# A decoder trunk on one core: the first projection fed with the raw input, transposed in column halves, and the norm applied afterwards

## The chip, the core and the metric

The kernel runs on one core of a Trainium2 chip. A core has five engines that run their own instruction queues side by side: TensorE (PE) for matrix products and transposes, VectorE (DVE), ScalarE (ACT), GpSimd (POOL), and SyncE (SP), which here issues most of the DMA transfers. They wait for each other by semaphores. The metric is the device time of one execution in microseconds (us); less is better. The median of the runs is what is compared.

## The reference

Two layers work on a residual stream of 512 tokens by 1024 features in float32. The first is a sandwich-normed dilated attention (three groups of four heads), then a gated convolutional FFN; the second is a forgetting attention on keys and values made once, and another FFN. What matters here is the very first step:

```python
def rms_norm(x, g):
    x32 = x.astype(jnp.float32)
    y = x32 * lax.rsqrt(jnp.mean(x32 * x32, axis=-1, keepdims=True) + EPS)
    return (y * g.astype(jnp.float32)).astype(x.dtype)
...
    mix = dilated_mixer(rms_norm(h, g[0]), w_qkv_a[l], w_o_a[l], cos, sin)
...
def dilated_mixer(xn, w_qkv, w_o, cos, sin):
    B, T, _ = xn.shape
    qkv = xn @ w_qkv
    q, k, v = jnp.split(qkv, 3, axis=-1)
    q = apply_rope(q.reshape(B, T, A_HEADS, HEAD_DIM), cos, sin)
    k = apply_rope(k.reshape(B, T, A_HEADS, HEAD_DIM), cos, sin)
```

The norm divides each token (a row of x) by its root mean square and multiplies each feature (a column) by a gain. The product with `w_qkv` sums over features. So the gain has to be in before the product, while the division by the row's root mean square may be done before it or on the product's rows.

## The kernel before

Products in float32 precision are made of three matmuls in a rounded float32 format: each operand is split into a high part (a cast on ScalarE) and a low part (the value minus the high part, on VectorE), and high·high, high·low and low·high are summed in PSUM (`mm3`, lines 276 to 279). Weights come in pieces of 128 x 1024 numbers, 512 KB each; `Weights.load` issues the DMAs on SP, `high` and `low` make the parts (lines 57 and 65, tiles `wearly` or `wraw` to `w`), `split(n)` does so up to piece n, and `get` hands one out and splits some pieces ahead (`ahead`).

The order of all work is written out by hand: the program's lines are issued in the order of the text, and each engine takes its own instructions in that order. Tokens come in four blocks of 128. The first projection of group 0's queries and keys (`qk0`, 512 output columns, pieces 0 to 3 of two feature chunks each) goes as follows. For each block b, `load_x` brings 512 KB; `rstd_h` squares it on ScalarE (line 284), takes the root (286) and the reciprocal on VectorE (288); `normed` multiplies by this and by the gain (296); `transpose_in` makes eight transposes on TensorE (345) and splits the result into `xah` and `xal` (348, 349). The gain as a row is spread over all partitions by four matmuls with a row of ones (`gain0`, line 260). Nine matmuls on zeros (`warm_up`, line 238) stand ahead of the first real ones. `qk_post` copies a block's queries and keys out of PSUM (1087) and POOL turns them by the rotary table (1093 to 1096). `reorder` makes on POOL a second copy of the transposed input, `xph` and `xpl`, with tokens in strides of four, for groups 1 and 2 (1076).

Behind this come `v_proj0`, the values of group 0 (weight pieces 4 and 5, 256 columns, tile `v_ps`), between whose halves the queries and keys are transposed (`qk_transpose`, line 1102, tile `qkT_ps`) and scored, then the products of groups 1 and 2 (`wide_proj`) on the reordered copy with attention steps between, the output projection, and the FFNs and the second layer, which take most of the time. POOL works through rotations and reordering in the order of the text, so a rotation stands behind each reordering that is issued before it.

The order of the text for the first projection was: block 0's norm, piece 0 split, block 0's transposes, piece 1 split, then block by block with further norms, transposes and splits put between the products.

Of the kernel before, what the change touches and what calls it, by code (L numbers as in the profile page):

```python
# [28 lines left out]
ND = NF // 2  # L29
LAST = 3  # L30
# [3 lines left out]
class Weights:  # L34
# [18 lines left out]
    def high(self, minus=False):  # L53
        if self.n_split < len(self.pieces):
            self.load(self.n_split + 1 + self.ahead_dma)
            raw, pair = self.raw.pop(self.n_split), self.new_pair()
            self.nc.scalar.copy(pair[:, 0], raw)  # L57
            if minus:
                self.nc.scalar.activation(pair[:, 1], raw, AF.Copy, scale=-1.0)
            self.half_done.append((raw, pair))  # L60

    def low(self):
        if self.half_done:
            raw, pair = self.half_done.pop()
            self.nc.vector.tensor_tensor(pair[:, 1], raw, pair[:, 0].bitcast(F32), ALU.subtract)  # L65
# [36 lines left out]
def trunk_kernel(ctx, tc, x, norm_gains, w_qkv_a, w_o_a, w_q_b, w_o_b, kv_norm, w_kvf, b_f,  # L102
# [38 lines left out]
    for g in range(3):  # L141
        for s in range(4):
            def f(raw, g=g, s=s):
                v = raw.rearrange("p (k c) -> p k c", k=2)
                return [(v[:, :, 0:256], cols(wqkv, 2 * s, 2, g * 256, 256)),
                        (v[:, :, 256:512], cols(wqkv, 2 * s, 2, 768 + g * 256, 256))]
            add(f)
# [69 lines left out]
    def load_x(b):  # L217
        sp.dma_start(h[:, b, :], xv[b * 128:(b + 1) * 128, :])
# [8 lines left out]
    g_row = t4([1, D], name="g_row")  # L227
    sp.dma_start(g_row, norm_gains[0:1, 0, :])
    ones = sml.tile([1, 128], F32R, tag="ones", name="ones", bufs=1)
    dve.memset(ones.bitcast(F32), 1.0)  # L230
# [16 lines left out]
    load_x(3)  # L247
# [5 lines left out]
    gr = t4([1, D], F32R, name="gain_h"), t4([1, D], F32R, name="gain_l")  # L253
    dve.tensor_copy(gr[0], g_row)
    dve.tensor_tensor(gr[1], g_row, gr[0].bitcast(F32), ALU.subtract)
    gain0 = [bank([128, 512], name="gain00") for _ in range(2)]
    warm_up(4)
    for part in range(2):
        for i in range(2):
            pe.matmul(gain0[i], ones, gr[part][:, i * 512:(i + 1) * 512], start=part == 0, stop=part == 1)  # L260
    warm_up(5)
# [7 lines left out]
    same = cst.tile([128, 4], F32, name="same")  # L269
    dve.tensor_reduce(same, ident.rearrange("p (a c) -> p c a", c=4), axis=mybir.AxisListType.X, op=ALU.add)  # L270
    dve.tensor_scalar(same, same, -NEG, NEG, ALU.mult, ALU.add)
    dve.tensor_tensor(mask2.rearrange("p (a c) -> p a c", c=4),
                      mask0[:, 128:256].rearrange("p (a c) -> p a c", c=4),
                      same[:, None, :].to_broadcast([128, 32, 4]), ALU.add)

# [5 lines left out]
    def rstd_h(b):  # L281
# [5 lines left out]
        r = small(1, "rs")  # L287
        dve.reciprocal(r, sd)
        return r

    H2 = (slice(0, 512), slice(512, 1024))
# [777 lines left out]
    def reorder(*blocks):  # L1069

        for i in range(2):
            for b in blocks:
                for part in range(2):
                    src = by_fourth(xT[part][i][:, :, b * 128:b * 128 + 128])
                    dst = xP[part][i].rearrange("p k (r l) -> p k r l", r=4)[:, :, :, b * 32:b * 32 + 32]
                    pool.tensor_copy(dst, src.bitcast(F32))
# [6 lines left out]
    def qk_post(g, b, o):  # L1083
# [3 lines left out]
        act.copy(qk.rearrange("p a d -> p (a d)"), o)  # L1087
# [162 lines left out]
    def norm0(b):  # L1250
        xn[b] = normed(b, rstd_h(b), gain0)

    def transpose0(b):
        transpose_in(b, xn.pop(b), xT)

    def qk0(b, *pieces):
        if b not in qk_banks:
            qk_banks[b] = bank([128, T], name="qk_ps")
        for s in pieces:
# [3 lines left out]
            for k in range(2):  # L1263
                kc = 2 * s + k
                ah, al = ax(0, b, kc)
                mm3(qk_banks[b], ah, al, wh[:, k, :], wl[:, k, :], kc == 0, kc == KD - 1)
# [24 lines left out]
    qk0(2, 2, 3)  # L1291
    W.split(5)
    qk_post(0, 2, qk_banks[2])
    qk0(3, 0, 1, 2, 3)
    W.ahead = 4
    W.split(6)
# [3 lines left out]
    reorder(2, 3)  # L1300
# [20 lines left out]
    def v_post(g, b, o):  # L1321
# [3 lines left out]
        act.copy(V[1][:, b, :], o[:, 0:256])  # L1325
        dve.tensor_copy(V[2][:, b, :], o[:, 256:512])
# [582 lines left out]
```

## Time and profile before

| | |
|---|---|
| median of 3 runs | 1109.95 us (1109.84 to 1110.57) |
| the profiled execution | 1110.27 us |
| its span, first to last instruction | 1108.5 us |
| TensorE busy | 1098.4 us, 99% of the span |
| VectorE, ScalarE, POOL busy | 81%, 60%, 20% |
| mean granted TensorE clock | 0.998 |

In the profile's rows a time is the start in us from the span's start, followed by how long it took; `L277` is line 277 of the kernel; `out<-in` names the tiles; `xN` counts instructions; a bracket at the end names the idle time before and what ended it. In rows of groups the numbers behind the bar are the busy time, the mean of one in ns, and the idle time before. In rows of stretches (`A:B`) the first number is the length, then the busy time and the count for TensorE, TensorE's weight loads, VectorE, ScalarE and POOL, then the granted clock, the DMA share and GB/s. Busy time of TensorE counts its work on zeros too, and its matmuls overlap in these rows: one is shown with 0.39 us where the next starts 0.23 us later.

### The profile page before, as it was taken

What the parts mean: (1) busy time and instruction counts of PE and PEld (TensorE: products, weight loads), DVE (VectorE), ACT (ScalarE), POOL (GpSimd) and SP (SyncE); (2) the same over time, 40 slices, a digit from 0 to 9 for tenths busy, and PEclk for the clock granted to TensorE, in tenths of its full rate; (3) what the DMA queues carried; (4) which work ended last, traced back from release to release, by engine and by line L of the source; (5) the groups of instructions that cost most, each with busy time, mean ns of one, the idle gap of its engine ahead of it and who ended that gap; (6) DMA issues with size and microseconds to landing.
All of it is one profiled execution on the core that took longest, in us unless ns stands there. A gap on an engine that the chain in (4) does not pass through costs nothing.

```text
span 1108.5 us, 18139 instructions
## 1 busy us (share of the span) xinstructions
PE 1098.4 (99%) x6611; PEld 948.4 (86%) x6611; DVE 896.6 (81%) x1494; ACT 660.2 (60%) x1092; POOL 222.2 (20%) x329
## 2 busy tenths in 40 slices
PE   9999999999999999999999999999999999999997
PEld 6988889889999988888888787789989999988886
DVE  6577878978887799997877777858978887799995
ACT  5444566566565547476555677756565565547473
POOL 1832100211111111000010766600211111111000
PEclk9999999999999999999999999999999999999999
DMA  9469864467789989885872677584467779999872
GB/s 325 149 207 408 346 171 132 108 134 196 176 201 216 256 318 341 295 310 108 210 153 76 193 222 211 161 246 124 114 133 191 181 200 219 249 315 340 306 247 77
DMA packets 184563, 237.32 MB, mean 214 GB/s; under 512 B 11737, under 2 KB 131529, under 8 KB 183962
## 3 DMA queue, kind: packets, MB, share of 16 engines
q1 hardware_dynamic: 166970, 176.61, 49.0%
q0 software_dynamic: 17504, 59.55, 23.3%
q8 instruction: 52, 0.85, 0.3%
q14 instruction: 37, 0.30, 0.1%
HBM read 170.28 MB, written 39.63 MB: 189 GB/s over the span
## 4 chain that ended last, share of the span: by engine, by line
PE 89%; DVE 3%; issue 3%; ACT 2%; DMA 2%; POOL 1%; DVEq 0%; POOLq 0%; ACTq 0%
PE up L278 13%; PE up L277 13%; PE up L279 13%; PE acc L278 8%; PE acc L277 8%; PE acc L279 8%; PE qk_ps L278 2%; PE qk_ps L277 2%; PE qk_ps L279 2%; PE first L279 1%; PE first L277 1%; PE first L278 1%; PE o_ps L1762 1%; PE pT_ps L1747 1%; PE v_ps L278 1%
## 5 line engine op out<-in xcount | busy, mean ns | idle before, releaser
L277 PE MATMUL acc<-w 128*128 128x512 f32 (+1 forms) x311 | 120.5, 388 | 0.0
L279 PE MATMUL acc<-w 128*128 128x512 f32 (+1 forms) x311 | 120.4, 387 | 0.0
L57 ACT CAST w<-wraw 128x1024 fp32r<-128x1024 f32 x96 | 99.0, 1048 | 9.5 <-issue 3.9
L278 PE MATMUL acc<-w 128*128 128x512 f32 (+1 forms) x267 | 103.2, 387 | 0.0
L65 DVE TENSOR_TENSOR w<-wraw,w 128x1024 fp32r<-128x1024 f32 x66 | 88.1, 1356 | 15.1 <-ACT w L57 14.7
L641 ACT ACTIVATE bb<-up,conv 128x512 f32<-128x512 f32 x80 | 60.0, 776 | 67.3 <-DVE up L1022 42.8
L278 PE MATMUL up<-xbl,w 128*128 128x512 f32 (+1 forms) x280 | 96.3, 344 | 0.0
L278 PE MATMUL up<-xcl,w 128*128 128x512 f32 (+1 forms) x280 | 96.3, 344 | 0.0
L277 PE MATMUL up<-xch,w 128*128 128x512 f32 (+1 forms) x280 | 96.3, 344 | 0.0
L277 PE MATMUL up<-xbh,w 128*128 128x512 f32 (+1 forms) x280 | 96.3, 344 | 0.0
L279 PE MATMUL up<-xbh,w 128*128 128x512 f32 (+1 forms) x280 | 96.2, 344 | 0.0
L279 PE MATMUL up<-xch,w 128*128 128x512 f32 (+1 forms) x280 | 96.2, 344 | 0.0
L277 PE MATMUL up<-xsh,w 128*128 128x256 f32 x320 | 90.6, 283 | 0.0
L278 PE MATMUL up<-xsl,w 128*128 128x256 f32 x320 | 90.6, 283 | 0.0
L279 PE MATMUL up<-xsh,w 128*128 128x256 f32 x320 | 90.6, 283 | 0.0
L277 PEld LDWEIGHTS acc<-w 128*128 128x128 f32 x311 | 58.4, 188 | 12.0
L279 PEld LDWEIGHTS acc<-w 128*128 128x128 f32 x311 | 58.4, 188 | 11.8
L644 DVE SCALAR_TENSOR_TENSOR bb<-up,conv,bb 128x510 f32<-128x510 f32 x80 | 59.9, 749 | 2.8
L642 DVE SCALAR_TENSOR_TENSOR bb<-up,conv,bb 128x511 f32<-128x511 f32 x80 | 59.4, 742 | 2.6 <-ACT bb L641 2.6
L277 PEld LDWEIGHTS up<-xsh,w 128*128 128x128 f32 x320 | 61.4, 192 | 0.0
L278 PEld LDWEIGHTS up<-xsl,w 128*128 128x128 f32 x320 | 61.4, 192 | 0.0
L279 PEld LDWEIGHTS up<-xsh,w 128*128 128x128 f32 x320 | 61.4, 192 | 0.0
(337 smaller groups left out, 3161.2 us busy)
## 6 DMA issues: line engine op xcount, KB each, us to landing
wraw<-in_w_up_dram SPq DMA_DIRECT2D x88, 512.0 KB, 5.0
w<-wraw POOLq DMA_DIRECT2D x50, 512.0 KB, 6.1
dT<-dsums SPq DMA_DIRECT2D x24, 512.0 KB, 6.0
hD<-hc POOLq DMA_DIRECT2D x44, 256.0 KB, 7.6
dact<-hD SPq DMA_DIRECT2D x44, 256.0 KB, 5.2
wraw<-dT SPq DMA_DIRECT2D x22, 512.0 KB, 6.6
wraw<-in_w_down_dram SPq DMA_DIRECT2D x22, 512.0 KB
dsums<-in_w_down_dram SPq DMA_DIRECT2D x18, 512.0 KB, 5.6
```

Of the source, the lines that this page charges most:

```text
L57: self.nc.scalar.copy(pair[:, 0], raw)
L65: self.nc.vector.tensor_tensor(pair[:, 1], raw, pair[:, 0].bitcast(F32), ALU.subtract)
L277: pe.matmul(o, ah, bh, start=first, stop=False, skip_group_check=shared)
L278: pe.matmul(o, ah, bl, start=False, stop=False, skip_group_check=shared)
L279: pe.matmul(o, al, bh, start=False, stop=last, skip_group_check=shared)
L641: act.activation(bb[:, s, :], ps, AF.Identity, bias=cp[:, 3, ch:ch + 1], scale=cp[:, 2, ch:ch + 1])
L642: dve.scalar_tensor_tensor(bb[:, s, 1:], ps[:, :T - 1], cp[:, 1, ch:ch + 1], bb[:, s, 1:], ALU.mult, ALU.add)
L644: dve.scalar_tensor_tensor(bb[:, s, 2:], ps[:, :T - 2], cp[:, 0, ch:ch + 1], bb[:, s, 2:], ALU.mult, ALU.add)
L1747: pe.transpose(o[:, k0 + k, :], p[:, hh, k * 128:(k + 1) * 128], ident)
L1762: pe.matmul(o[64 * hh:64 * hh + 64, i * 128:(i + 1) * 128], Vt[hd // 8][:, k, (hd % 8) * 64:(hd % 8) * 64 + 64], pT[j, i, hh][:, k, :], st ...
```

## The change

The first projection now takes the raw input. x is loaded and transposed in column halves (`load_x(b, i)`, `transpose0(b, i)`: four transposes of `h` itself). The gain comes in as eight rows of 128 and is turned by one transpose into a column per feature chunk (`gain0`, 128 x 8). When a half-block leaves PSUM, the gain is applied as a scale per partition, one instruction of 128 x 128 for each of the four chunks on ScalarE (the high part) and on VectorE (the low part): `split0`. Each row's reciprocal root mean square goes into a column of `r0` (`rstd0`) and is applied where the products leave PSUM: in `qk_post`, in `v_proj0` and in `v_post`. Groups 1 and 2 need these scales in the strided token order, `r1`: POOL's queue writes `r0` to DRAM and reads it back.

The order is new as well. The first halves of all blocks and pieces 0 and 1 go first: the products of pieces 0 and 1 on blocks 0 to 3, then those of pieces 2 and 3. Within a piece the three products are ordered by operand and no longer by chunk. Pieces 0 and 1 are loaded and split in two halves by chunk. `reorder` is called by column half, the first half of all blocks ahead of all rotations, the second behind them. The four gain matmuls are gone, and the five later warm-up matmuls stand behind the first four transposes.

```diff
@@ class Weights
-            self.nc.scalar.copy(pair[:, 0], raw)
+            for s in HALVES[self.n_split < 2]:
+                self.nc.scalar.copy(pair[:, 0, s], raw[:, s])
...
-            self.nc.vector.tensor_tensor(pair[:, 1], raw, pair[:, 0].bitcast(F32), ALU.subtract)
+            for s in HALVES[self.n_split < 2]:
+                self.nc.vector.tensor_tensor(pair[:, 1, s], raw[:, s], pair[:, 0, s].bitcast(F32), ALU.subtract)
@@ loads
-    load_x(0)
+    load_x(0, 0)
+    sp.dma_start(g_rows, norm_gains[0, 0].rearrange("(k p) -> k p", p=128))
     W.load(2)
-    load_x(1)
+    load_x(1, 0)
+    load_x(2, 0)
+    load_x(3, 0)
     W.load(3)
-    load_x(2)
+    load_x(0, 1)
     W.load(4)
+    for b in range(1, 4):
+        load_x(b, 1)
@@ gain
-    gr = t4([1, D], F32R, name="gain_h"), t4([1, D], F32R, name="gain_l")
-    dve.tensor_copy(gr[0], g_row)
-    dve.tensor_tensor(gr[1], g_row, gr[0].bitcast(F32), ALU.subtract)
-    gain0 = [bank([128, 512], name="gain00") for _ in range(2)]
-    warm_up(4)
-    for part in range(2):
-        for i in range(2):
-            pe.matmul(gain0[i], ones, gr[part][:, i * 512:(i + 1) * 512], start=part == 0, stop=part == 1)
-    warm_up(5)
+    gain0 = sml.tile([128, 8], F32, tag="gain0", name="gain0", bufs=1)
+    warm_up(WARM[0])
+    g0_ps = bank([128, 8], name="g0_ps")
+    pe.transpose(g0_ps, g_rows, ident[:8, :8])
+    dve.tensor_copy(gain0, g0_ps)
@@ evictions
-        act.copy(qk.rearrange("p a d -> p (a d)"), o)
+        act.activation(qk.rearrange("p a d -> p (a d)"), o, AF.Copy, scale=scale_of(g, b))
...
-                act.copy(V[0][:, b - 1:b + 1, :], banks[b // 2])
+                for i in range(2):
+                    act.activation(V[0][:, b - 1 + i, :], banks[b // 2][:, i], AF.Copy, scale=scale_of(0, b - 1 + i))
@@ the first projection
+    def transpose0(b, i):
+        n = 2 if (b, i) == (0, 0) else 4
+        for k0 in range(0, 4, n):
+            pt = bank([128, n, 128], name="xt_ps")
+            for k in range(n):
+                c = (4 * i + k0 + k) * 128
+                pe.transpose(pt[:, k, :], h[:, b, c:c + 128], ident)
+                x_ps[b, 4 * i + k0 + k] = pt[:, k, :]
+
+    def split0(b, i, ks=range(4)):
+        s = slice(b * 128, b * 128 + 128)
+        parts = [(xT[0][i][:, k, s], xT[1][i][:, k, s], x_ps.pop((b, 4 * i + k)),
+                  gain0[:, 4 * i + k:4 * i + k + 1]) for k in ks]
+        for hi, lo, o, g in parts:
+            act.activation(hi, o, AF.Copy, scale=g)
+        for hi, lo, o, g in parts:
+            dve.scalar_tensor_tensor(lo, o, g, hi.bitcast(F32), ALU.mult, ALU.subtract)
...
+            for x, w in ((0, wh), (1, wh), (0, wl)):
+                for k in range(2):
+                    kc = 2 * s + k
+                    pe.matmul(o, ax(0, b, kc)[x], w[:, k, :], start=kc == 0 and x == 0 and w is wh,
+                              stop=kc == KD - 1 and w is wl)
...
-    norm0(0)
+    transpose0(0, 0)
+    warm_up(WARM[1])
+    split0(0, 0, (0, 1))
     W.split(1)
-    transpose0(0)
+    split0(0, 0, (2, 3))
     W.split(2)
     qk0(0, 0)
-    norm0(1)
+    x0(1, 0)
     qk0(0, 1)
+    x0(2, 0)
+    qk0(1, 0)
     W.split(3)
-    transpose0(1)
-    qk0(0, 2)
-    norm0(2)
-    qk0(1, 0)
+    qk0(1, 1)
+    x0(3, 0)
+    qk0(2, 0, 1)
     W.split(4)
-    qk0(1, 1, 2)
-    transpose0(2)
-    qk0(0, 3)
-    norm0(3)
-    qk0(1, 3)
+    x0(0, 1)
...
+    qk0(3, 0, 1)
+    x0(1, 1)
+    rstd0(0)
+    reorder(0, 3, 0, 1, 2)
+    qk0(0, 2, 3)
+    x0(2, 1)
     qk_post(0, 0, qk_banks[0])
+    qk0(1, 2, 3)
+    rstd0(1)
+    x0(3, 1)
+    W.split(5)
     qk_post(0, 1, qk_banks[1])
-    reorder(0, 1)
-    qk0(2, 0, 1)
-    transpose0(3)
+    rstd0(2)
     qk0(2, 2, 3)
-    W.split(5)
+    W.split(6)
+    rstd0(3)
     qk_post(0, 2, qk_banks[2])
-    qk0(3, 0, 1, 2, 3)
+    qk0(3, 2, 3)
     W.ahead = 4
-    W.split(6)
     qk_post(0, 3, qk_banks[3])
     sums = down_sums([(1, 6), (1, 7)], in_two, sp, 1, 3)
     next(sums)
-    reorder(2, 3)
+    pool.dma_start(rd.rearrange("(b p) o -> p (b o)", p=128), r0)
+    reorder(1, 0, 1, 2, 3)
+    pool.dma_start(r1, rd.rearrange("(l r) o -> l (r o)", r=4))
```

`x0(b, i)` is `transpose0(b, i)` followed by `split0(b, i)`; `WARM` is (4, 5); `HALVES` gives two halves of 512 columns for pieces 0 and 1 and the whole for the others. Rows without times in the prediction show the instructions as each engine's queue holds them, with the semaphores that they wait for.

More of the change, by code (lines that the diff above doesn't have):

```diff
@@ L226, in trunk_kernel @@
     dve.memset(eps_t, EPS)
[L227 to L230, printed above, removed]
+    g_rows = t2([8, 128], name="g0_rows")
     zero = t2([128, 512], BF16, name="zero")
@@ L286, in rstd_h @@
         act.activation(sd, ss, AF.Sqrt, bias=eps_t)
[L287 removed]
+        r = small(1, "rs") if r is None else r
         dve.reciprocal(r, sd)
         return r
[L291 removed]
     def normed(b, r, gain):
@@ L1067, in by_fourth, with scale_of, reorder @@
         return a.rearrange(spec, r=4)
[L1069 to L1076, printed above, removed]
+    r0 = sml.tile([128, 4], F32, tag="r0", name="r0", bufs=1)
+    r1 = sml.tile([128, 4], F32, tag="r1", name="r1", bufs=1)
+    rd = tc.dram_tile([T, 1], F32, name="rd")
+    def scale_of(g, b):
+        return (r1 if g else r0)[:, b:b + 1]
+    def reorder(i, *blocks):
+        for b in blocks:
+            for part in range(2):
+                src = by_fourth(xT[part][i][:, :, b * 128:b * 128 + 128])
+                dst = xP[part][i].rearrange("p k (r l) -> p k r l", r=4)[:, :, :, b * 32:b * 32 + 32]
+                pool.tensor_copy(dst, src.bitcast(F32))
     def ax(g, b, kc):
```

45 lines of the change are left out of this document (25 added, 20 removed).

## The prediction

> **What bounds the kernel now.** The page first: one engine carries the span.
>
> ```profile
> span 1108.5 us, 18139 instructions
> PE 1098.4 (99%) x6611; PEld 948.4 (86%) x6611; DVE 896.6 (81%) x1494; ACT 660.2 (60%) x1092; POOL 222.2 (20%) x329
> ```
>
> TensorE is busy for all but 10 us. So time can go only where it does no useful work, and the busy row hides such work at the start, where it runs on zeros. Then the chain of waits for the first 16 us, and the timeline around the hand-over from this projection to the value projection.
>
> ```profile
> 1.36 1.89 PE warm L238 x4
> 3.24 2.24 PE gain L260 x4
> 5.48 2.25 PE warm L238 x5
> 7.73 1.65 PE xt_ps L345 x8
> ...
> 9.42 0.46 issue
> 9.88 1.05 ACT w L57
> 10.94 1.05 ACT junk L284 x2
> ...
> 12.01 0.30 ACT sd L286
> ...
> 13.21 0.74 DVE xn L296
> 13.95 1.15 DVE w L65
> ...
> 15.14 0.50 PE qk_ps L278
> ```
> ```profile
> 9.28 0.50 PE L277 MATMUL qk_ps<-w,xah 128*128 128x512 f32 x1
> ...
> 20.53 1.03 PE L345 MATMUL xt_ps<-ident,xn 128*128 128x128 f32 x8
> ...
> 35.47 0.39 PE L278 MATMUL qk_ps<-w,xah 128*128 128x512 f32 x1
> 35.70 0.39 PE L279 MATMUL qk_ps<-w,xal 128*128 128x512 f32 x1
> 35.92 0.28 PE L277 MATMUL v_ps<-w,xah 128*128 128x256 f32 x1
> 36.04 0.28 PE L278 MATMUL v_ps<-w,xah 128*128 128x256 f32 x1
> ...
> 41.68 1.03 PE L1102 MATMUL qkT_ps<-ident,qk 128*128 128x128 f32 x8
> ```
> ```profile
> 15.20:36.10 20.90, 20.90 (x101) 17.45 (x102) 11.22 (x15) 9.40 (x17) 11.78 (x15) 1.00 0.73 241
> ```
>
> The reader is to see three things. Until 9.28 no matmul of the projection runs; until 15.14 the end is set by ScalarE and VectorE, which take turns at squares, norms and splits. From 15.2 to 36.1 (the row by itself: stretch, TensorE busy) TensorE is full. And the projection ends at 35.92, where the value projection starts; 5.76 us later, at 41.68, come the first transposes of queries and keys. From there on nothing stops TensorE until the tail, so what the first 36 us save is carried to the end, unless a new wait eats it.
>
> **The change part by part.** The work of the projection on TensorE stays: 96 matmuls of 512 columns, 0.2275 us apart (35.47 to 35.70, rounded), 21.84 us, and 32 transposes at about 0.11 us ((1.03 − 0.27) / 7). Reordering the three products inside a piece costs nothing by that rate. So the question is when the stream starts and what interrupts it.
>
> *Arrival of x.*
>
> ```profile
> 0.74 0.35 SPq L228 DMA_DIRECT2D g_row<-in_norm_gains_dram  x1
> 1.15 0.35 SPq L218 DMA_DIRECT2D h<-in_x_dram  x1
> 4.85 1.06 ACT L284 ACTIVATE junk<-h 128x1024 bf16<-128x1024 f32 x1 [2.61 <-DMA h<-in_x_dram]
> ```
> ```profile
> 2.50:5.00 2.50, 2.50 (x6) 0.99 (x4) 2.32 (x5) 0.15 (x1) 0.00 (x0) 1.00 0.85 308
> 10.00:16.00 6.00, 4.99 (x24) 3.52 (x24) 5.54 (x8) 5.06 (x8) 0.00 (x0) 1.00 1.06 378
> ```
>
> The first block, 512 KB, was issued at 1.15 and waited for until 4.85. Now half of it is asked for, 0.41 us earlier (in g_row's place, 0.74), and 256 KB less at 308 GB/s (last column) is 0.85 us: it is there at 3.6. The gain rows, 4 KB behind it, I put at 3.75. Behind them one transfer of 256 KB lands each 0.85 us at first, 0.7 later: the halves of piece 0 at 4.5 and 5.3, of piece 1 at 6.1 and 6.9, x of blocks 1 to 3 by 9. All 4.1 MB are in by about 15, as before; SP's three added issues of 0.35 us are faster than what they wait behind.
>
> *Start of TensorE.* These are the rows of order ahead of the first matmuls, before and now:
>
> ```order
> L260 MATMUL gain_116<-gain_h,ones 128x512 [waits DVE_49]
> L260 MATMUL gain_117<-gain_h,ones 128x512
> L260 MATMUL gain_116<-gain_l,ones 128x512 [waits DVE_49]
> L260 MATMUL gain_117<-gain_l,ones 128x512
> L238 LDWEIGHTS zero
> L238 MATMUL warm<-zero 128x512
> ...
> L345 MATMUL xt_ps<-ident,xn 128x128 [waits DVE_49,Pool_49]
> L345 MATMUL xt_ps<-ident,xn 128x128 x3
> ...
> L277 MATMUL qk_ps<-w,xah_146 128x512 [waits Activation_49]
> ```
> ```order
> L267 MATMUL g_ps<-ident,g_rows 128x8 [waits DMAHW1_49,Pool_49]
> L1263 MATMUL xt_ps<-ident,h 128x128 [waits DMAHW0_49]
> L1263 MATMUL xt_ps<-ident,h 128x128 x3
> L245 LDWEIGHTS zero
> L245 MATMUL warm<-zero 128x512
> ...
> L1290 MATMUL qk_ps<-w,xah_133 128x512 [waits Activation_49] x2
> L1290 MATMUL qk_ps<-w,xal_135 128x512 [waits DVE_49] x2
> L1290 MATMUL qk_ps<-w,xah_133 128x512 [waits DVE_49] x2
> L1263 MATMUL xt_ps<-ident,h 128x128 [waits DMAHW6_49]
> ```
>
> The gain broadcast (four matmuls, 2.24 us of the chain) and the wait for a normalized block leave; the raw transposes wait for a DMA alone and stand ahead of the five warm-ups. Early on TensorE runs at half its later rate:
>
> ```profile
> 5.42 2.31 PE L238 MATMUL warm<-zero 128*128 128x512 bf16 x5
> 7.53 1.84 PE L345 MATMUL xt_ps<-ident,xn 128*128 128x128 f32 x8
> ```
>
> Eight transposes span 1.84 us here and 1.03 at 20.53; warm-ups stand 0.43 apart, though the granted clock reads 1.00 throughout. By 9.28 the rate is full. So: gain transpose at 3.75, four transposes to 4.8, five warm-ups of 0.43 to 7.0. I take 7.05 for the first projection matmul. Before, full rate came some 3.8 us after the five warm-ups began (5.42); here that would be 8.6; I take 9.15, the place it had.
>
> Are its operands there? Prices:
>
> ```profile
> L1154 ACT COPY PT<-pT_ps x4: 266/278/299, 56.9 to 57.4; 128x128 f32<-128x128 f32 x4
> ```
> ```profile
> L821 ACT CAST w<-dt 128x512 fp32r<-128x512 f32 x22 | 13.6, 618 | 1.8 <-DMA dt<-dT 1.6
> ...
> L1113 ACT ACTIVATE p<-p,st 128x128 f32<-128x128 f32 x36 | 14.0, 394 | 9.0 <-DVE st L1112 8.9
> ...
> L534 ACT ACTIVATE xqh<-nT,gcol 128x512 fp32r<-128x512 f32 x8 | 5.1, 716 | 0.0
> ...
> L348 ACT CAST xah<-xt_ps 128x512 fp32r<-128x512 f32 x8 | 4.4, 589 | 7.9 <-PE xt_ps L345 7.9
> ```
> ```profile
> L535 DVE SCALAR_TENSOR_TENSOR xql<-nT,gcol,xqh 128x512 fp32r<-128x512 f32 x8 | 5.5, 747 | 0.0
> ...
> L1112 DVE CUSTOM_DVE_ANT_0 p<-s_ps,mask 128x128 f32<-128x128 f32 x36 | 8.0, 286 | 1.9 <-PE s_ps L1129 1.9
> ```
>
> No row is a 128x128 copy out of PSUM with a scale per partition. Below: a plain one stands about 0.17 us from the next (four start between 56.9 and 57.4). Above: 0.39 (L1113). The scale adds 0.10 (716 against 618), so I take 0.27, nearer to L1154, which is the same copy but for the scale; a half-block on ScalarE then costs 1.08 us where one cast cost 0.59. On VectorE one of the four takes between 0.2 (L1112, less its overlap) and 0.33; I take 0.26, 512-column L535 less 384 columns. A half piece is 0.52 there and 0.62 on VectorE, half of the chain's 1.05 and of the 1.22 below. With ScalarE free at 4.9, two splits, piece 0 and two more end at 7.2, piece 1 at 8.2; VectorE has the low part of piece 0 at 7.5 and of piece 1 at 9.3. TensorE wants them at 7.05, 8.8 and 10.7: all in time.
>
> *The stream.* From 7.05: 21.84 us of matmuls and 28 transposes, 3.05. Half rate until 9.15, as before: 2.1 us do 4.9 matmuls instead of 9.2, a loss of 1.0. One stall I find by going through the queues: block 1's transposes end at 9.8, ScalarE's four at 11.1, VectorE's four at 12.3, TensorE asks at 12.0: 0.3. Later half-blocks are ready 0.3 to 2 us ahead. Sum: 7.05 + 21.84 + 3.05 + 1.0 + 0.3 = 33.25, against 35.92: **2.65 us earlier**.
>
> *What moved behind it.* The squares and roots (10.94 to 12.31 in the chain, 1.35 us a block on ScalarE) now stand among late splits, ahead of the casts of pieces 4 and 5:
>
> ```order
> L1271 ACTIVATE xah_134<-xt_ps,gain_114 128x128 [waits PE_49]
> L1271 ACTIVATE xah_134<-xt_ps,gain_114 128x128 x3
> L60 CAST w<-wearly 128x1024 [waits DMAHW2_49]
> L1091 ACTIVATE qk_343<-qk_ps,r_141 128x512 [waits DVE_49]
> L284 ACTIVATE junk,s_393<-h 128x1024 [waits DMAHW7_49]
> L286 ACTIVATE sd<-s_393,eps_t 128x1 [waits Activation_49]
> L60 CAST w<-wearly 128x1024 [waits DMAHW3_49]
> ```
>
> This is ScalarE's queue now, near 29 us; before, both casts stood there without squares between. Piece 5 is cast by 33.0, its low part by 34.3; the value projection wants it after 12 matmuls of 0.12 us (35.92 to 36.04), at 34.8: covered by 0.5. On POOL the first halves' reordering (8 casts) goes ahead of all rotations, the second halves' behind them, with two small DMAs for the scales in the strided order, which the first grouped projection needs only after its last product, some 20 us later. The scaled evictions add about 0.1 us each on ScalarE, off the path. The masks' three small instructions fall into VectorE's idle time near 21.
>
> The sum is against the profiled execution, 1110.27; the median of the runs lies 0.32 lower, 1109.95. 1109.95 − 2.65 = **1107.3 us**.
>
> **A rule weighed.** The Trainium skill, "TensorE: Matmul & The Clock Gate", Part 1, says that the array starts at half rate and goes to full after a busy window of about 3.4 us whose phase is free. The rows above do not show it counted from 1.36, since 9.03 was still slow; counted from the warm-ups at 5.42 it fits. By that rule the full rate comes between 8.2 and 11.6 here (4.8 + 3.4, plus up to one window), and my sum would read 3.1 down to 1.8 us instead of 2.65.
>
> **The rivals.** *A, full rate comes before the first real matmul.* For it: nothing breaks the stream from 4.0 on. Against: before, TensorE was at work from 1.36 and still slow at 8.8. It gives back the 1.0: 1106.3.
>
> *B, half rate lasts until about 12.5.* Counted from 7.05, when the warm-ups end, 3.8 us lead to 10.9; counted from behind the transposes that break the stream (10.5 at half rate), to 14.3; I take the middle. Each us costs 0.47 (1 − 0.2275/0.43): 1.6 more, less the stall it hides: gain 1.4, 1108.6. For it: the gap from 3.25 to 3.75 and the short instructions; against: the warm-ups stand together as before. (The same page says, in Part 4, that transposes do not count as work for the clock; that would favour B.)
>
> *C, ScalarE becomes the bound.* At 0.39 a split the late half-blocks miss TensorE by 0.2 to 0.5, and if the low part of piece 5 takes 1.97 instead of 1.22, as one did beside POOL (below), the value projection waits 0.9: gain 1.0, 1108.95. Against: the PSUM copy row.
>
> *D, slower: the rotations come too late.* In place of rotations first, POOL's queue now starts with the reordering, ahead of the first block's rotation (tu):
>
> ```order
> L1080 CAST xph_137<-xah_133 128x16x32 [waits Activation_49]
> L1080 CAST xpl_139<-xal_135 128x16x32 [waits DVE_49]
> L1080 CAST xph_137<-xah_133 128x16x32
> L1080 CAST xpl_139<-xal_135 128x16x32
> ...
> L1097 TENSOR_TENSOR tu<-qk_343,rope 128x128 [waits DMAHW1_49,Activation_49]
> ```
> ```order
> L1096 TENSOR_TENSOR qk_302<-tu 128x8x16 [waits Pool_49]
> L1076 CAST xph_150<-xah_146 128x16x32
> L1076 CAST xpl_152<-xal_148 128x16x32 [waits DVE_49]
> L1076 CAST xph_150<-xah_146 128x16x32
> L1076 CAST xpl_152<-xal_148 128x16x32 [waits DVE_49]
> ```
> ```profile
> 13.86 1.22 DVE L65 TENSOR_TENSOR w<-wearly,w 128x1024 fp32r<-128x1024 f32 x1
> ...
> 29.55 1.97 DVE L65 TENSOR_TENSOR w<-wearly,w 128x1024 fp32r<-128x1024 f32 x1
> ```
> ```profile
> 28.27 1.13 POOL L1076 CAST xpl<-xal 128x512 fp32r<-128x512 f32 x1
> ...
> 30.37 2.12 POOL L1076 CAST xpl<-xal 128x512 fp32r<-128x512 f32 x1
> ...
> 38.05 1.30 POOL L1094 TENSOR_TENSOR tu<-qk,rope 128x64 f32<-128x64 f32 x1
> ```
>
> The first order fence is now: eight casts, then the rotations. The second is before: the rotations of blocks 0 and 1, then casts. A cast takes 1.1 us, and 2.1 while VectorE runs L65; rotation steps then take 1.3. If all paid the high price from 17.6 on: 8 × 2.1 + 8 × 1.3 = 27.2, the second block is turned at 44.8, while TensorE asks at 39.5: it stands 5.3 us, 1112.6. It decides from 42.2 on. Against: only weight splits showed that price, and few fall into this stretch; at the low price the second block is done by 33.
>
> **How the numbers follow.** The forecast's own case (gain 1.9 to 3.2) gets 0.50, A 0.18, B 0.13, C 0.08, D 0.05; 0.06 is for what I do not see, half of it slower. The range goes from A with data a little earlier still (gain 4.1, 1105.8) to B and C together (gain 0.4, 1109.6). A measurement of this kernel tells about 0.2%, 2.2 us, from no change; 1107.73 is that bound, and 0.35 of the forecast's 0.50 lies beyond it. Faster: 0.35 + 0.18 + 0.03 = 0.56; same: 0.15 + 0.13 + 0.08 = 0.36; slower: 0.05 + 0.03 = 0.08.
>
> **What would show it.** First projection matmul near 7.05, value projection at 33.3, first transposes of queries and keys at 39.05. Right for the clock: matmuls 0.43 apart until about 9.15. C would show as waits of value matmuls for VectorE's split, D as transposes waiting for POOL. Wrong altogether if the raw x lands no earlier than 4.8, or if a later stage opens waits that were not there.

## The result, and the profile after

The changed kernel takes 1106.95 us in the median (7 runs, 1106.44 to 1107.10), beside 1110.21 for the kernel before: a ratio of 0.997, 95% interval 0.996 to 0.9981. Measured again later, beside other runs of the kernel before, it took 1106.85 (0.9969, 0.9957 to 0.9981). The prediction was 1107.3. The gain is 3.3 us where 2.65 was forecast.

The head of the page of the changed kernel:

```profile
span 1105.0 us, 18176 instructions
PE 1096.0 (99%) x6608; PEld 948.5 (86%) x6608; DVE 894.8 (81%) x1510; ACT 667.4 (60%) x1120; POOL 222.7 (20%) x331
```

TensorE is still busy for all but 9 us, but with 2.4 us less of it. What has gone is the gain broadcast, four matmuls of 2.24 us, for which one short transpose of 0.24 came in (6608 matmuls instead of 6611). The nine matmuls on zeros are all still there, and so is the work of the projection. The chain of waits at the start (start, duration, what):

```profile
0.74 0.39 SPq L228
1.19 2.32 DMA g_rows<-in_norm_gains_dram
...
3.65 0.24 PE g_ps L267
3.89 1.05 PE xt_ps L1263 x4
4.94 2.13 PE warm L245 x5
7.07 2.56 PE qk_ps L1290 x6
9.63 0.52 PE xt_ps L1263 x4
10.15 1.38 PE qk_ps L1290 x6
...
11.97 2.76 PE qk_ps L1290 x12
```

Before, ScalarE and VectorE stood in this chain until 15.14. Now nothing but TensorE stands in it after the gain rows have landed. Six matmuls take 2.56 us at first and 1.38 from 10.15 on: that is the change from half to full rate. The trace's record of the granted clock puts it at 9.67; the record begins there, so that stretches before it are shown with 1.00. Every time given below for full rate is read from this record. TensorE's own rows in the timeline of the changed kernel show the same and the two marks that the prediction named:

```profile
4.73 2.34 PE L245 MATMUL warm<-zero 128*128 128x512 bf16 x5
6.51 1.42 PE L1290 MATMUL qk_ps<-w,xah 128*128 128x512 f32 x2
7.72 1.05 PE L1290 MATMUL qk_ps<-w,xal 128*128 128x512 f32 x2
8.57 1.05 PE L1290 MATMUL qk_ps<-w,xah 128*128 128x512 f32 x2
9.43 0.72 PE L1263 MATMUL xt_ps<-ident,h 128*128 128x128 f32 x4
...
10.45 0.63 PE L1290 MATMUL qk_ps<-w,xal 128*128 128x512 f32 x2
...
33.30 0.28 PE L277 MATMUL v_ps<-w,xah 128*128 128x256 f32 x1
...
39.05 1.04 PE L1106 MATMUL qkT_ps<-ident,qk 128*128 128x128 f32 x8
```

No row of TensorE from 4.73 to the end of this stretch has a bracket, so it does not stand there. The value projection starts at 33.30 (before 35.92), the first transposes of queries and keys at 39.05 (before 41.68).

Matched matmul by matmul, the lead of TensorE over the kernel before is 2.62 us at 40 us and 2.67 at 550 us. Then it grows in two places, to 3.1 by 582 us and to 4.05 by 634 us, where the kernel before waits and the changed one does not. The rows of the kernel before are:

```profile
582.43 0.50 PE L278 MATMUL v_ps<-w,xkh 128*128 128x512 f32 x1 [0.17 <-DVE w L1537]
...
633.99 0.50 PE L279 MATMUL q_ps<-xqh,w 128*128 128x512 f32 x1 [0.83 <-DMA w<-wraw]
```

At the end 0.6 us are given back: the last output transfers are issued 4.07 us earlier than before, but the span is only 3.5 shorter. The two rows, first of the kernel before, then of the changed one (start, duration of four issues):

```profile
1101.58 4.12 SPq L547 DMA_DIRECT2D out_dram<-h  x4
```
```profile
1097.51 4.12 SPq L545 DMA_DIRECT2D out_dram<-h  x4
```

So the books of these two profiles are 2.62 from the projection, 1.45 late in the program and minus 0.6 at the end. The forecast had the first and knew nothing of the last two. That the first agrees to 0.03 us is luck of this profile: the same kernel profiled again had a lead of 3.08 there.

### The profile page after: what moved, and what is told of

Read it like the earlier page. It is cut to its first block, busy times and chain, and to the rows that moved or that the text cites. A ratio compares the mean times of both kernels' runs of the same rounds, so it can differ in the third digit from the quotient of the medians.

```text
span 1105.0 us, 18176 instructions
## 1 busy us (share of the span) xinstructions
PE 1096.0 (99%) x6608; PEld 948.5 (86%) x6608; DVE 894.8 (81%) x1510; ACT 667.4 (60%) x1120; POOL 222.7 (20%) x331
## 4 chain that ended last, share of the span: by engine, by line
PE 96%; ACT 2%; DVE 1%; issue 0%; DMA 0%; DVEq 0%; SPq 0%; ACTq 0%
PE up L277 13%; PE up L278 13%; PE up L279 13%; PE acc L277 8%; PE acc L278 8%; PE acc L279 8%; PE qk_ps L1290 2%; PE v_ps L277 2%; PE v_ps L278 2%; PE v_ps L279 2%; PE s_ps L1759 1%; PE o_ps L1806 1%; PE q_ps L277 1%; PE first L279 1%; PE first L277 1%; PE first L278 1%
```

## The experiments

**The order of before, with the raw input.** Is the gain due to the raw input alone, or does the new order carry part of it? The loads, norms, rotations and reorderings go back to the order of before too; the diff is shortened to the first calls.

```diff
-    x0(1, 0); qk0(0, 1); x0(2, 0); qk0(1, 0); ...
+    x0(0, 1); qk0(0, 1); W.split(3); x0(1, 0); x0(1, 1)
+    qk0(0, 2); qk0(1, 0); W.split(4); qk0(1, 1, 2); ...
```

> Raw input, halves and norm at the eviction stay; loads and work go block by block again, as before the change. Theory S (the gain is the earlier start, and the new order keeps the stream unbroken): first projection matmul at 7.05 to 7.10 as in the changed kernel, but the value projection at 34.4 instead of 33.30, since TensorE waits about 0.9 us for the high part of block 0's second half at piece 2 and 0.4 us for its low part; median 1108.1. Rival R (the raw input alone does it, the order is worth nothing): value projection at 33.2 to 33.4, median 1107.0. Rival O (the order does it, the early start is lost in waits without it): value projection at 35.5 or later, median 1109.3 or more.

1108.45 us (0.9983, 0.9974 to 0.9993); first transposes of queries and keys at 39.74. In the projection TensorE waits once, and not for the split that I had named. Its timeline, ScalarE's and TensorE's rows:

```profile
11.54 1.04 ACT L60 CAST w<-wearly 128x1024 fp32r<-128x1024 f32 x1 [0.67 <-DMA wearly<-in_w_qkv_a_dram]
12.49 2.17 ACT L1272 ACTIVATE xah<-xt_ps,gain 128x128 fp32r<-128x128 f32 x8
...
12.63 0.73 PE L1291 MATMUL qk_ps<-w,xah 128*128 128x512 f32 x2 [0.70 <-ACT w L60]
```

Block by block, piece 2 is wanted as the third piece, and it lands only at 11.5: TensorE stands 0.70 for its cast. The new order works on two pieces for some 14 us and needs no third one in that time. This run had the full rate a microsecond earlier than the profile of the changed kernel (8.71 against 9.67); beside a run with the same clock (38.69 at 8.76, under "One DMA less" below) the old order costs 1.05 us. So R and O fall: of the lead that the projection then has, 3.0 us, about two thirds are the raw input's and a third the order's. By the medians the old order keeps 1.8 us of the 3.3 (1110.26 for the kernel before beside it). S had the split between the two about right, but not its mechanism: TensorE waited for the load of a weight piece, not for the split of x, and the value projection came at 33.99, not at 34.4.

**Pieces 0 and 1 whole.**

```diff
-HALVES = (slice(0, 1024),), (slice(0, 512), slice(512, 1024))
+HALVES = (slice(0, 1024),), (slice(0, 1024),)
```

> Pieces 0 and 1 are loaded, cast and split whole instead of in two halves; all else as changed. Theory S: the warm-ups, which end at 7.05, hide it (piece 0 landed at 5.77 in the changed kernel, a whole cast of 1.05 us ends at 6.85): first projection matmul at 7.0 to 7.2, value projection at 33.3 to 33.4. Rival H (the halves are what lets the stream start early): first matmul at 7.5 or later, value projection at 33.6 to 33.9.

The edit makes the cast and the subtraction whole; the loads stay as they are, four transfers for the two pieces in both kernels. One run, 1107.94; value projection at 33.74. The timeline:

```profile
6.00 1.04 ACT L60 CAST w<-wearly 128x1024 fp32r<-128x1024 f32 x1 [0.86 <-DMA wearly<-in_w_qkv_a_dram]
...
7.09 1.22 PE L1290 MATMUL qk_ps<-w,xah 128*128 128x512 f32 x2
...
9.95 0.66 PE L1263 MATMUL xt_ps<-ident,h 128*128 128x128 f32 x4 [0.43 <-DMA h<-in_x_dram]
```

The whole piece is cast at 7.04, a quarter of a microsecond behind the warm-ups' end; 0.43 more is a wait for x of block 1, which landed at 9.9 here and at 9.1 in the changed kernel. S is wrong by the size of the first. The second is taken for the load's own variation: the edit does not touch the loads, and in the other profiles with the same loads TensorE took up this x between 9.0 and 9.7. H named 33.6 to 33.9 and is right by that number, but not by its first matmul (7.5 or later). One run cannot part the two further. The start is that close to its loads.

**Fewer warm-ups: three, and none, behind the first transposes.**

```diff
-WARM = 4, 5
+WARM = 4, 3        # the other kernel: 4, 0
```

> Three warm-up matmuls instead of five behind the first transposes. First projection matmul at about 6.6 instead of 7.07, limited by the first halves of piece 0. Theory F (full rate comes at about the same time after the first work of TensorE, whatever the work is): spacing changes from 0.43 to 0.23 at 9.7, value projection at 33.15 to 33.25. Theory W (full rate is counted from the real work, or a shorter unbroken run of long matmuls delays it): spacing changes at 10.4 or later, value projection at 33.5 to 33.7.

> No warm-up matmuls behind the first transposes; TensorE stands idle from about 4.9 until the first split and the first half of piece 0 are there, about 6.6. Theory F (full rate comes at about the same time after the first work): spacing changes from 0.43 to 0.23 at 9.7, value projection at 33.15 to 33.25, median 1106.8. Theory W (the idle time starts the count anew): spacing changes about 3.8 to 6.5 us behind 6.6, at 10.4 to 13.1, value projection at 33.7 to 34.8, median 1107.4 to 1108.5.

Three: one run, 1109.34, value projection at 35.28. None: 1107.94 (0.9981, 0.9971 to 0.999), its ten runs lying between 1106.89 and 1110.62. TensorE's timeline with three:

```profile
8.30 1.05 PE L1290 MATMUL qk_ps<-w,xah 128*128 128x512 f32 x2
9.71 1.11 PE L1263 MATMUL xt_ps<-ident,h 128*128 128x128 f32 x4 [0.35 <-DMA h<-in_x_dram]
...
11.48 1.05 PE L1290 MATMUL qk_ps<-w,xal 128*128 128x512 f32 x2
12.33 1.05 PE L1290 MATMUL qk_ps<-w,xah 128*128 128x512 f32 x2
13.18 0.78 PE L1263 MATMUL xt_ps<-ident,h 128*128 128x128 f32 x4
13.71 0.71 PE L1290 MATMUL qk_ps<-w,xah 128*128 128x512 f32 x2
```

Pairs of matmuls span 1.05 us until 13: half rate lasts to 13.5, though the first projection matmul stands 0.36 earlier (6.15 against 6.51). TensorE reaches block 1 before its x is there, stands 0.35, and full rate comes 3.8 us behind that wait. With none it stood twice 0.8 for casts of piece 0, the last until 7.35, and got full rate at 10.27. Theory F falls. W has the direction and, without warm-ups, the time (value projection at 33.70, median in its range); with three its value projection (33.5 to 33.7) is 1.6 us too early, since full rate came later than it allowed for. The five warm-ups are worth 1.0 us in the median (1107.94 against 1106.95). The runs without them also lie further apart, over 3.7 us against 0.7 in the 13 runs of the changed kernel; but 1.9 of the 3.7 is a single run, and other kernels with five warm-ups spread over 0.65 to 1.5, so a steadier time is suggested and not shown.

**The changed kernel again, and one more early warm-up.** The first has no edit; the second:

```diff
-WARM = 4, 5
+WARM = 5, 5
```

> The changed kernel again, to be compared with the two kernels beside it, and to see whether its profile's later part repeats. Theory B (the 0.9 to 1.4 us that every variant so far gains on the kernel before between 570 and 640 us come with the change): TensorE's lead over the kernel before grows between 570 and 640 by 0.9 to 1.4 us here too, median 1106.7 to 1107.2. Rival J (chance waits of one profile of the kernel before): the lead stays at 2.0 to 3.0 us up to the end and the median gain is 2.6.

> One more warm-up matmul in the first group, so that TensorE is busy without a gap from 1.23 us on (in the changed kernel it stands 0.53 us before the gain rows). Theory U (full rate comes at the end of the first window of 3.41 us, of free phase, in which TensorE did not stand): spacing changes from 0.43 to 0.23 between 4.7 and 8.1 instead of between 7.3 and 10.7; the first projection matmul stays at 7.05, and the value projection comes at 32.9 to 33.2, held back by the landing of x of block 1 at 9.1 to 9.7; median 0.1 to 0.4 us under the changed kernel's. Rival N (warm-ups ahead of the transposes count for nothing): spacing changes between 7.3 and 10.7 as before, value projection at 33.3, no difference.

Again: 1106.85, full rate at 8.17, first transposes of queries and keys at 38.60, no wait at 582 or 634, and the lead grows by 1.36 between 570 and 640: theory B's numbers hold. The lead is still taken against the one profile of the kernel before, so this run cannot rule out J; two later profiles of the old projection do that for 634 (below). With the early warm-up: 1107.28 (0.9973, 0.9963 to 0.9983), no gain. Its timeline:

```profile
7.28 0.50 PE L1290 MATMUL qk_ps<-w,xah 128*128 128x512 f32 x1 [0.81 <-ACT w L60]
...
8.09 0.63 PE L1290 MATMUL qk_ps<-w,xah 128*128 128x512 f32 x2
9.73 0.66 PE L1263 MATMUL xt_ps<-ident,h 128*128 128x128 f32 x4 [1.01 <-DMA h<-in_x_dram]
```

Pairs span 0.63 from the start: full rate came at 5.34, as theory U said, 4.3 us earlier than in the first profile of the changed kernel. TensorE then stands 0.81 for a cast of piece 0 and 1.01 for x of block 1, and the value projection comes at 33.52, not at U's 32.9 to 33.2. What the clock gives, the loads take back. So the forecast's question of when full rate comes decides less than it seemed. Between 9.67 and 8.17 an earlier full rate still moved the value projection (33.30 in the first profile, 32.84 in the repeated one); with 6.98 and 5.34 it came no earlier than that (33.08 and 33.52), because x of block 1 arrives at 9.0 to 9.9.

**The late gain: the pool of buffers.** The change takes three tiles less from the pool of ten 4 KB buffers, so every later tile of this pool stands in another buffer, and behind another release. Is that why the waits at 582 and 634 are gone?

```diff
     make_identity(nc, ident)
+    for i in range(3):          # in the kernel before: range(7)
+        pool.memset(t4([1, 8], name="spare"), 0.0)
```

> The changed kernel with three small tiles more taken at the start from the pool of ten 4 KB buffers (it lost three tiles of this pool by the change), each set by one tiny instruction: later tiles of this pool stand in the same buffers as in the kernel before. Theory P (the gain of 0.9 to 1.4 us between 570 and 640 comes from the rotation of this pool, which sets when the second load of ck may start): second load of ck 3.0 us behind the first instead of 5.8, waits for weights return there, the lead over the kernel before stays at 2.6 us from 100 us to the end; median 1107.9 to 1108.4. Rival T (it comes from the earlier start or from something else in the change): lead grows to 3.5 to 4.1 us, median 1106.7 to 1107.2.

> The kernel before with seven small tiles more taken at the start from the same pool of ten, so that later tiles stand in the buffers that they have in the changed kernel; nothing of the projection is changed. Theory P: no lead up to 570 us, then 0.9 to 1.4 us by 640; less about 0.0 to 0.6 at the end, median 1108.8 to 1109.5. Rival T: no lead anywhere, median 1110.0 to 1110.4.

The changed kernel with the rotation of before: 1107.46 (0.9973, 0.9963 to 0.9982); the second load of ck stays 5.8 us behind the first, TensorE waits 0.16 at 630, and its lead grows from 2.8 at 570 to 3.96 at 634 and falls to 3.7 by 800. The kernel before with the rotation of after: 1110.37 (1.0, 0.999 to 1.0009), with this wait:

```profile
634.36 0.50 PE L281 MATMUL q_ps<-xqh,w 128*128 128x512 f32 x1 [1.01 <-DMA w<-wraw]
```

As the cause of the gain at 634, theory P falls on both sides. But T's median is missed as well: it lies between the two ranges, 0.6 us above the changed kernel's (1106.85, run beside it), and the runs of the two do not overlap. Of this, 0.35 is there at 40 us already in the two profiles (lead 2.73 against 3.08), the rest comes from 630 on. And the kernel before with the rotation of after has no wait at 582 and gains 0.45 us there on the profile of before. The changed kernel with the rotation of before does not get this wait back, while the kernel before with two more DMAs (below) has it again:

```profile
582.57 0.50 PE L278 MATMUL v_ps<-w,xkh 128*128 128x512 f32 x1 [0.19 <-DVE w L1543]
```

So the wait at 582 stands in two of three profiles of the old projection and in none of the eleven of the new one. What removes it is open.

**The late gain: POOL's queue of DMAs.** Matched like the matmuls, POOL's DMAs show single hold-ups of 0.8 to 1.2 us, at three places among the last 86 DMAs of each kernel, and not at the same ones. In the kernel before one hits the copy that TensorE waits for at 634, in the changed kernel a transfer of sums. POOL's timeline, before and then after:

```profile
611.49 0.58 POOL L615 DMA_DIRECT2D dT<-dsums  x1 [0.77 <-DVE dsums L608]
...
627.59 0.94 POOL L82 DMA_DIRECT2D w<-wraw  x1 [0.93 <-ACT bias L1725]
```
```profile
609.14 1.20 POOL L613 DMA_DIRECT2D dT<-dsums  x2 [1.56 <-DVE dsums L607]
...
623.65 0.91 POOL L86 DMA_DIRECT2D w<-wraw  x1
...
629.99 1.51 POOL L1740 TENSOR_SCALAR bias<-ck,cq 128x512 f32<-128x512 f32 x2 [0.70 <-DMA w<-wraw]
```

The change adds two DMAs to this queue (the scales go to DRAM and back). So these two, and a small tile for them, went into the kernel before (the diff is shortened):

```diff
     next(sums)
+    pool.memset(r0, 1.0)
+    pool.dma_start(rd.rearrange("(b p) o -> p (b o)", p=128), r0)
     reorder(2, 3)
+    pool.dma_start(r1, rd.rearrange("(l r) o -> l (r o)", r=4))
```

> The kernel before with two DMAs more on POOL's queue: a small tile of ones is written to DRAM and read back, in the shapes and at the place in which the changed kernel passes its scales. Nothing reads what comes back. Theory Q (now and then one DMA issued by POOL is held up by 0.8 to 1.2 us, and which one it is depends on the DMAs that POOL has issued before it; in the kernel before it hits the copy w<-wraw at 627.6 that TensorE waits for at 634, in the changed kernel the transfer dT<-dsums behind cd<-c, for which nobody waits): the copy w<-wraw near 627.6 comes without its 0.9 us, the first dT<-dsums near 611.5 comes 0.8 us later, TensorE's wait of 0.8 at q_ps falls to 0.2 or less, median 1109.2 to 1109.7. Rival T (it takes the rest of the change): hold-up and wait stay where they are, median 1110.2 to 1110.6.

1110.85 (1.0003, 0.9994 to 1.0013): no gain. POOL's rows, and TensorE's among them:

```profile
612.42 1.21 POOL L615 DMA_DIRECT2D dT<-dsums  x2 [1.56 <-DVE dsums L609]
...
626.96 0.91 POOL L82 DMA_DIRECT2D w<-wraw  x1
...
634.38 0.50 PE L279 MATMUL q_ps<-xqh,w 128*128 128x512 f32 x1 [1.08 <-DMA w<-wraw]
```

The hold-up moved just as Q said: the two transfers of sums go out together, the copy goes out without delay. Yet TensorE waits 1.08. The copy took 7.4 us to land here and 6.2 in the changed kernel (issued 623.65, waited for until 629.9); over the eleven profiles of the changed projection it is 6.1 to 6.7. In the two other profiles of the old projection it is 6.4 and 6.5, not longer, but there the copy goes out 0.93 and 0.92 late (the second is the kernel before with the rotation of after):

```profile
627.81 0.94 POOL L82 DMA_DIRECT2D w<-wraw  x1 [0.92 <-ACT bias L1727]
```

So in these two the hold-up accounts for the wait by its size. In the third the hold-up is gone, and a slower transfer of the same size stands in its place. Two small DMAs shift the hold-up, but taking it off the copy was not enough. Why that one transfer was slow is not shown. In the packets of its trace a fetch of instructions, 16 KB from 632.06 to 633.0, lies just ahead of the copy's end; in the changed kernels it comes behind it, and in the two other old profiles it lies in the middle of a copy that was not slow. Whether it matters was not tested. Eleven profiles of kernels with the changed projection show TensorE's wait as 0 to 0.4 us, three with the old one as 0.8 to 1.1. It goes with the change; which part of the change removes it stays open.

**One DMA less.** At the end of the program SP waits in turn for the eight semaphores that its DMAs use in rotation, and for others beside them. The changed kernel issues 481 DMAs on SP and the one before 477. So in the changed kernel the last output transfer has the first semaphore of the eight: in the trace the wait for it ends at 1103.3, and the seven that follow run on to 1104.1. Before, three followed.

```diff
-    for b in range(1, 4):
-        load_x(b, 1)
+    load_x(1, 1)
+    sp.dma_start(h[:, 2:4, H2[1]], xv[256:512, H2[1]].rearrange("(b p) c -> p b c", p=128))
```

> The changed kernel with the last two loads of x (second halves of blocks 2 and 3) joined into one DMA, so that SP issues 480 DMAs instead of 481. Theory E (the eight semaphores of SP's DMAs are used in turn and awaited in a fixed order at the end, so the end costs more where the last output DMA has an early one; here it gets the last): from the last output DMA's landing to the end of the span 1.0 to 1.1 us instead of 1.72, median 1106.1 to 1106.4. Rival L (the longer end comes from somewhere else, or the joined load lands too late for block 2's second half): end as in the changed kernel or a new wait of TensorE near 24 us, median 1106.8 or more.

1106.30 (5 runs, 1105.20 to 1106.74; 0.9962, 0.995 to 0.9975), the fastest of all kernels here. The output rows of this kernel:

```profile
1097.28 4.12 SPq L545 DMA_DIRECT2D out_dram<-h  x4
```

Its span is 1104.0: from these issues to the end 6.7 us instead of 7.5. From the last landing to the end it is 0.91 instead of 1.72 (before 1.09). Theory E holds, with an end a little shorter than its 1.0 to 1.1. By time alone this kernel is hard to tell from the changed one, since their runs overlap; the 0.8 us at the end of the profile is what shows it.

**POOL's queue made longer.**

```diff
+    reorder(0, 3, 0, 1, 2)
+    reorder(0, 3, 0, 1, 2)
     reorder(0, 3, 0, 1, 2)
```

> POOL does the eight casts of the first halves three times instead of once, 16 casts of 1.1 us more ahead of the rotations. Theory D (POOL's queue has about 6 us of room there, from 32.9, when the second block is turned, to 39.05, when TensorE asks): second block turned near 48, TensorE stands 8 to 10 us at the first transposes of queries and keys, time 1115 to 1117. Rival F (TensorE does not depend on POOL's queue there): no wait at these transposes, time 1106.7 to 1107.5.

One run, 1120.07. The timeline, POOL's last steps for block 1 and TensorE:

```profile
49.06 1.11 PE L1106 MATMUL qkT_ps<-ident,qk 128*128 128x128 f32 x4 [10.08 <-POOL qk L1100]
...
50.05 0.45 POOL L1100 TENSOR_TENSOR qk<-tu 128x128 f32<-128x128 f32 x1
...
50.56 1.11 PE L1106 MATMUL qkT_ps<-ident,qk 128*128 128x128 f32 x4 [0.38 <-POOL qk L1100]
...
51.68 0.41 PE L278 MATMUL v_ps<-w,xah 128*128 128x256 f32 x1
...
54.84 0.28 PE L278 MATMUL v_ps<-w,xah 128*128 128x256 f32 x1
```

TensorE does depend on POOL there: the second block is turned at 50.50 instead of 32.86, and TensorE stands 10.5 us. So D's mechanism is right, and so is its estimate of some 6 us of room; the expectation had 48, 8 to 10 us and 1115 to 1117. Five of the casts from 31 us on took 2.1 us instead of 1.1, so both prices of D occur. The rest of the 13.1 us is the clock, which the expectation did not have: the record shows half rate from 41.11, during the wait, to 54.77. Value matmuls are 0.21 apart after the wait and 0.12 again from 54.8, and 5.7 us at a loss of 0.46 are 2.6. Here the long wait cost TensorE its full rate.

**No gain.** One cast and one subtraction per half-block, the gain left out.

```diff
-        for hi, lo, o, g in parts:
-            act.activation(hi, o, AF.Copy, scale=g)
-        for hi, lo, o, g in parts:
-            dve.scalar_tensor_tensor(lo, o, g, hi.bitcast(F32), ALU.mult, ALU.subtract)
+        act.copy(hi4, p4)
+        dve.tensor_tensor(lo4, p4, hi4.bitcast(F32), ALU.subtract)
```

> The gain is left out of the first projection's input (a different result): the high part of a half-block is one cast of 128x512 on ScalarE and the low part one subtraction on VectorE instead of four scaled instructions each. Theory S (neither engine bounds the stream): no change but for the clock, so the value projection starts at 33.3 plus 0.47 us for each us by which full rate comes later than 9.67 (less where it comes earlier), time 1106.6 to 1107.3. Rival C (ScalarE's and VectorE's splits bound the stream): value projection 0.5 to 2 us earlier than that, time 1105.0 to 1106.4.

One run, 1107.16; full rate at 9.08, value projection at 33.20. S gives 33.30 − 0.47 × 0.59 = 33.02, so it is not even earlier, but 0.18 later. The four scaled instructions did not hold TensorE up, and rival C is out.

## Why the prediction was right, and where it was not

*The first 33 us.* The value projection was put at 33.25 and started at 33.30, the transposes of queries and keys at 39.05 and 39.05. The mechanism is right: the start, the unbroken stream and the room behind it came as forecast. The sum is right too, but several of its terms are not:

- Start: 7.05 forecast, 7.07 in the chain. By spacing (five warm-ups of 0.427 from 4.73) the stream begins at 6.87. The raw x and the gain rows were in time, as said: the gain is turned at 3.65 and four transposes span 1.05.
- Half rate: 1.0 forecast, until 9.15; in this profile it lasted until 9.67, which is 2.8 us at a loss of 0.46 a microsecond, 1.3. The repeated run had full rate at 8.17. The forecast took the place that it had in the kernel before; it has no fixed place.
- One stall of 0.3 at block 1: there was none. The step that failed here is "VectorE's four at 12.3, TensorE asks at 12.0". A product of one piece needs two chunks, not four, and VectorE had finished these two in time.
- Matmuls: 0.2275 apart forecast, 0.23 measured (12 in 2.76), 0.24 us in all.

6.87 + 22.08 + 3.08 + 1.28 makes 33.31. The errors (-0.18, +0.3, -0.3, +0.24) cancel, and that is luck: the same kernel profiled again started the value projection at 32.84, 0.4 us ahead of the sum. Partly it is more than luck, since what full rate costs when it comes late, TensorE would else lose in part by waiting for x.

*Around it.* ScalarE's four took 1.14 and VectorE's four 1.13 (1.08 and 1.04 forecast); piece 5 was split at 34.24 (34.3), wanted at 34.8, and no value matmul waited; POOL had turned the second block at 32.86 ("done by 33"). These rows of the changed kernel's timeline show the last two:

```profile
32.40 0.46 POOL L1100 TENSOR_TENSOR qk<-tu 128x128 f32<-128x128 f32 x1
...
33.01 1.23 DVE L69 TENSOR_TENSOR w<-wearly,w 128x1024 fp32r<-128x1024 f32 x1 [0.77 <-ACT w L60]
```

*The rivals.* In eight profiles with the warm-ups of the changed kernel full rate came between 6.98 and 9.67, so B did not occur; with three warm-ups, in one run, it came at 13.54, so the rival was no idle one. A did, nearly, in the run with POOL's longer queue (6.98, and the stream begins at 6.87), and gave no more than 0.2 us on the value projection (33.08), because TensorE then stood 0.8 for x of block 1: the rival's time left that load out. C falls with the kernel without gain, D is a true mechanism that stayed 6 us away.

*What was missed.* "From there on nothing stops TensorE until the tail, so what the first 36 us save is carried to the end" is the step that failed. The profile of the kernel before has waits behind 41 us that the sentence denies: 0.17 at 582, 0.83 at 634 and 0.77 at 707. The changed kernel has only the last of them, and gained 1.4 us around the first two, cause open. And 0.6 was lost at the end: the forecast counts three added issues on SP where there are four (eight half loads of x for four), and prices them by their issue alone, not by the semaphore that the last DMA then has. The two were of opposite sign and left 0.8 us of gain that the forecast did not have, inside its range by that size and not by its account.

*The rule weighed.* The Trainium skill, "TensorE: Matmul & The Clock Gate", Part 1, has the array go to full rate after a busy window of about 3.4 us (3413 ns) of free phase. The traces agree: full rate lasts from 9.14 to 1104.82 before and from 9.67 to 1101.94 after, 321 and 320 of these windows, and in the other profiles too every stretch of it is a whole number of them. With the changed kernel's warm-ups it began between 6.98 and 9.67; by that rule it lies between about 7 and 10.5, an estimate from the page's window counted from the end of the last wait at 3.6. With no warm-ups full rate came 2.9 us after the last wait, which is less than one window; there the trace differs. What Part 4 says of transposes, that they do not count as busy in the same way, is not borne out here: in the kernel before with the seven spare tiles the window that ended at 10.64 held more transposes (1.8 us) than matmuls (1.3), and full rate followed. Matmuls alone cannot well be what counts, since with three warm-ups the window that ended at 10.13 (13.54 less 3.41) held 2.65 us of them and did not bring it. The two windows had the same idle time (0.36 and 0.35), so what does count stays open.

## What to carry to other kernels

If a normalization stands ahead of a projection and its scale is one number per row, let the projection run on the raw input and scale its output: the start then depends on loads and one split, and the loop order should be chosen so that the fewest different operands are needed while loads are still arriving. Once the stream is unbroken, look at what it is close to before you push it further: here a faster clock only met the next load. And count the DMAs that an edit adds or removes on each queue, since here the end of the program cost 0.8 us more or less by that number.

## What had not been expected of the hardware

- An earlier full rate was worth something only while the loads kept up: 0.46 us on the value projection from 9.67 to 8.17, nothing more at 6.98 and 5.34.
- A few of POOL's DMAs, three places among the last 86, are issued 0.8 to 1.2 us late. Seven small POOL instructions more did not move this, two DMAs more did.
- A wait of 10 us cost TensorE its full rate (one run): it was lost at 41.1, 2 us into the wait, and came back at 54.8, 5.7 us after the wait ended.
- From the last output's landing to the end of the span it is 0.91, 1.09 or 1.72 us, by the semaphore that the last DMA happens to have.
